# Sums of weight blocks in a seven-product scheme: accumulating transfers in place of VectorE additions

## The chip, the cores and the metric

One NeuronCore of a Trainium2 chip runs the whole kernel. The time is the device time of one execution in microseconds, the median of the runs on the chip. Beside the runs one execution was taken by the hardware profiler; its trace gives the span from the first to the last instruction, and the busy and idle time of each engine: PE (TensorE), PEld (its weight loads), DVE (VectorE), ACT (ScalarE), POOL (GpSimd), and SP, which here only issues transfers.

## The reference

A decoder layer on 528 positions (16 meta tokens and 512 tokens) of width 2048, all in float32:

```python
xn = rmsnorm(h, g_pre)
p = xn @ w_in                       # 2048 x 7184 columns
q, k, v, z_gla, r, hc, gate_b, gate_c, z_conv = jnp.split(p, SPLIT_POINTS, axis=-1)
log_a = jax.nn.log_sigmoid(r @ w_gate_up + b_gate) / GATE_TAU
o = gla_chunked(q * GLA_HEAD_K ** -0.5, k, v, log_a)     # 4 heads, chunks of 64 positions
y_gla = rmsnorm(o, g_gla_out) * silu(z_gla)
y_conv = gate_b * causal_dwconv(gate_c * hc, w_conv) * silu(z_conv)
y = jnp.concatenate([y_gla, y_conv], axis=-1) @ w_out
out = (h + rmsnorm(y, g_post))[N_META:]
```

Most of the arithmetic is in the product with `w_in`, and the next largest part in that with `w_out`.

## The kernel before

**Splitting.** Float32 operands are multiplied in three passes. `split` makes two tiles of a raw block: `whi`, a cast on ACT (L124), and `wlo`, the raw block less `whi`, on DVE (L125). Then TensorE multiplies high by high, high by low and low by high. There are three buffers of `whi` and of `wlo`.

**Pairs.** The columns of `w_in` lie in DRAM as tiles of 128 columns (`w_t`). After some plain products at the start, the rest is done by 25 objects `Pair`: two tiles of 128 columns (such as h4 and c4, whose PSUM tiles are named `h4c4P...`) against all of `xn`, by a scheme of seven block products instead of eight. A pair has four blocks of weights of 128 x 1024 float32, 512 KB each: `"11"` and `"12"`, the halves over the contraction of the first tile, and `"21"` and `"22"`, those of the second. The seven products are made in the order P5, P1, P6, P2, P3, P7, P4, each of 24 matmuls (8 steps of contraction by three passes). Their weight operands are sums of blocks:

- P5: 21 + 22
- P1: 11
- P6: 11 + 21 + 22
- P2: 12
- P3: 11 + 12 + 21 + 22
- P7: 11 + 21
- P4: 22

The sums of `xn` on the other side are made once, ahead of the pairs. The pairs stand in this order: nine for z, k, q and v, then h0c0 and b0s0 (in these eleven the work of the gated attention, the "stages", is interleaved), then fourteen more for the convolution group, h1c1, b1s1 to h7c7, b7s7. Then comes `w_out`: `Whole` and six `Out`, which have their own sums of blocks.

**Slots and loads.** Raw blocks lie in five slots. `load_free` issues the next load of the list on SP's queue whenever a slot is free; `free` gives a slot back once the last instruction that reads it has been written. Four blocks of a pair and the first of the next pair are held when a pair begins.

**Order of the work.** `line` lists all products. The main loop prepares two products ahead (`AHEAD = 2`): `prepare_next` calls `Pair.prepare`, which issues the additions and the split of one product; `multiply` issues its matmuls; `away` takes finished products out of PSUM with copies on ACT and subtractions on DVE. Each engine runs its instructions in the order in which the program, after the framework's scheduling, has written them. In `prepare`, three sums are made by `add` on DVE (L200) and the fourth by a subtraction (L230), all in place in the raw slots:

```python
if name == "P5":   add(raw["21"], raw["22"])
elif name == "P6": add(raw["11"], raw["21"])
elif name == "P3": add(raw["12"], raw["11"])
elif name == "P7": raw["11"] = raw["11"] - raw["22"]     # L230
```

POOL does a few memsets, masks and one small product, and issues no transfers.

Of the kernel before, what the change touches and what calls it, by code (L numbers as in the profile page):

```python
# [13 lines left out]
ALU = mybir.AluOpType  # L14
# [18 lines left out]
NB = 8  # L33
# [12 lines left out]
def hymba_kernel(ctx, tc, xT, x, g_pre, w_r, w_t, w_up, b_gate, g_gla, w_conv, w_o, g_post, out):  # L46
    nc = tc.nc
# [17 lines left out]
    V, A, G = nc.vector, nc.scalar, nc.gpsimd  # L65
# [54 lines left out]
    def split(raw, shape, pool=None):  # L120
        pool = pool or wp
        hi = pool.tile(shape, F32R, tag="whi", name="whi")
        lo = pool.tile(shape, F32R, tag="wlo", name="wlo")
        A.copy(hi, raw)  # L124
        V.tensor_tensor(out=lo, in0=raw, in1=hi.bitcast(F32), op=ALU.subtract)  # L125
        return hi, lo
# [5 lines left out]
    def new_raw(shape=None):  # L132
        tag = slots.pop(0)
        t = wp.tile(shape or [P, NB, P], F32, tag=tag, name="raw", bufs=1)
        held[id(t)] = (t, tag)
        return t

    def free(t):
        slots.append(held.pop(id(t))[1])
# [47 lines left out]
    line = []  # L187
    ready = []
# [10 lines left out]
    def add(a, b):  # L199
        V.tensor_tensor(out=a, in0=a, in1=b, op=ALU.add)  # L200

    class Pair:
# [6 lines left out]
                line.append((self, name, name == ORDER[-1]))  # L209
            loads.extend((self, b) for b in self.blocks)  # L210

        def load(self, b):

            r = self.raw[b] = new_raw()
            g = NB * (b in ("12", "22"))
            i = TILE[self.na if b[0] == "1" else self.nb]
            nc.sync.dma_start(r, w_t[i][:, g:g + NB, :])

        blocks = ("21", "22", "11", "12")

        def prepare(self, name):
            raw = self.raw
            if name == "P5":
                add(raw["21"], raw["22"])
            elif name == "P6":
                add(raw["11"], raw["21"])
            elif name == "P3":
                add(raw["12"], raw["11"])
            elif name == "P7":
                V.tensor_tensor(out=raw["11"], in0=raw["11"], in1=raw["22"], op=ALU.subtract)  # L230
            b = {"P5": "21", "P1": "11", "P6": "11", "P2": "12", "P3": "12", "P7": "11",
                 "P4": "22"}[name]
            two = split(raw[b], [P, NB, P])
            if name in ("P6", "P3", "P7", "P4"):
                free(raw[{"P6": "21", "P3": "12", "P7": "11", "P4": "22"}[name]])
            return two

        def multiply(self, name, two):
# [53 lines left out]
    def load_free():  # L292
        while slots and loads:
            p, b = loads.pop(0)
            p.load(b)

    def prepare_next():
        p, name, last = line[len(ready)]
        load_free()
        ready.append(p.prepare(name))  # L300
        load_free()

# [347 lines left out]
    with tc.tile_pool(name="ini", bufs=1, reuse_waits="tile") as ini:  # L650
# [13 lines left out]
        for n_, (k0, k1) in enumerate(XCUT):  # L664
            ks = slice(k0, k1)
            nc.sync.dma_start(xr[:, ks, :], xT[:, ks, :])
            for kt in range(k0, k1):
                xt, xk = raw_x(kt)
                src = xr[:, kt, :].rearrange("p (s t) -> p s t", t=XHALF)
                A.activation(xt[0][:, :, xk, :], src, AF.Copy, scale=gp[:, kt:kt + 1])  # L670
                V.scalar_tensor_tensor(out=xt[1][:, :, xk, :], in0=src, scalar=gp[:, kt:kt + 1],
                                       in1=xt[0][:, :, xk, :].bitcast(F32),
# [7 lines left out]
            if k0 == 0:  # L680
# [3 lines left out]
                                in1=wr2[:, :, 0:RANK].bitcast(F32), op=ALU.subtract)  # L684
# [28 lines left out]
        for raw in (wk[1][2], wq_[0][2], wq_[1][2]):  # L713
# [5 lines left out]
                        op=ALU.subtract)  # L719
# [35 lines left out]
        def want_plain(n):  # L755
            if n in plain and n not in grans:
# [9 lines left out]
                        op=ALU.subtract)  # L766
# [51 lines left out]
        free(stage[0])  # L818
        all_pairs()
        prepare_next()  # L820
        prepare_next()
        block("P1", xa, 0, b11)
        block("P4", xa, 1, tt)
        multiply(0)
        prepare_next()
        block("P2", xb, 0, b21)
        multiply(1)
# [241 lines left out]
```

## Time and profile before

| | |
|---|---|
| median of 3 runs | 821.43 us (820.8 to 821.86) |
| profiled execution | 823.31 us, span 820.8 us |
| granted TensorE clock, mean | 0.990 |
| busy: PE, DVE, ACT, POOL | 794.0, 688.4, 437.6, 3.8 us |
| moved by DMA | 98.97 MB, mean 121 GB/s |
| 512 KB loads of `w_t` | 108, median 4.1 us from issue to landing |
| stages: start and plain products; 25 pairs; `w_out` | 0 to 99; 99 to 639; 639 to 821 us |

In the rows of groups, the first number after the bar is the busy time of all instructions of the group, then the mean of one in ns; after the second bar stands the idle time of the engine just before them and what ended most of it. In rows of the chain and the timeline the first number is the start in us, the second the length. A row names the line, the engine, the operation, and output and inputs; `x168` is a count.

### The profile page before, as it was taken

The page shows a single profiled execution, that of the slowest core. Times are in us where ns is not written, and L with a number is a line of the kernel's source. Part 1 is how long each engine was busy: PE and PEld are TensorE (multiplying, and loading weights), DVE is VectorE, ACT ScalarE, POOL GpSimd, SP SyncE. Part 2 cuts the span into 40 slices and gives each one's busy share as a digit, 9 for nine tenths or more (in the row PEclk, how much of TensorE's full clock was granted, in tenths as well). Part 3 has the DMA queues.
Part 4 walks back from the last instruction along what each step waited for, and adds up shares of the span by engine and source line. Part 5 has one row for each costly group of instructions (what it writes and reads, how often), then busy time and mean ns, then how long its engine had stood idle before and what let it go on. Part 6 is the DMA issues. An engine that isn't in the chain of part 4 may idle for free.

```text
span 820.8 us, 15178 instructions
## 1 busy us (share of the span) xinstructions
PE 794.0 (97%) x6364; PEld 776.2 (95%) x6364; DVE 688.4 (84%) x820; ACT 437.6 (53%) x638; POOL 3.8 (0%) x15
## 2 busy tenths in 40 slices
PE   9999989999999999999999999999999999999992
PEld 8999989998999999999999999999999889999992
DVE  6999979789697789878887888787879986787887
ACT  7635675685766484644444444444446534444442
POOL 0000000000000000000000000000000000000000
PEclk9999999999999999999999999999999999999996
DMA  9513243234133532253333333333333622333346
GB/s 288 223 52 91 92 129 102 89 119 154 54 103 114 169 99 88 85 193 103 111 105 119 100 116 106 115 102 110 105 115 116 178 77 76 104 101 106 103 161 250
DMA packets 34052, 98.97 MB, mean 121 GB/s; under 512 B 4064, under 2 KB 8800, under 8 KB 33344
## 3 DMA queue, kind: packets, MB, share of 16 engines
q1 hardware_dynamic: 31968, 94.73, 35.7%
q10 hardware_dynamic: 2016, 3.29, 1.2%
q8 instruction: 49, 0.80, 0.4%
q14 instruction: 19, 0.16, 0.1%
HBM read 89.61 MB, written 8.39 MB: 119 GB/s over the span
## 4 chain that ended last, share of the span: by engine, by line
PE 77%; DVE 12%; DMA 4%; ACT 4%; issue 2%; SPq 0%; DVEq 0%; ACTq 0%
PE out L63 5%; PE out3P L63 4%; PE out1P L63 4%; PE out2P L63 3%; PE v L63 3%; PE v2v3P L63 3%; PE h0c0P L63 2%; PE h5c5P L63 2%; PE h2c2P L63 2%; PE h7c7P L63 2%; PE h6c6P L63 2%; PE h4c4P L63 2%; PE h3c3P L63 2%; PE h1c1P L63 2%; PE b0s0P L63 2%; PE b6s6P L63 2%
## 5 line engine op out<-in xcount | busy, mean ns | idle before, releaser
L124 ACT CAST whi<-raw 128x1024 fp32r<-128x1024 f32 x225 | 235.2, 1050 | 256.7 <-DVE raw L200 85.4
L125 DVE TENSOR_TENSOR wlo<-raw,whi 128x1024 fp32r<-128x1024 f32 x225 | 273.7, 1220 | 66.7 <-ACT whi L124 61.5
L200 DVE TENSOR_TENSOR raw<-raw 128x1024 f32<-128x1024 f32 x75 | 90.3, 1219 | 6.6 <-DMA raw<-in_w_t_dram 5.6
L230 DVE TENSOR_TENSOR raw<-raw 128x1024 f32<-128x1024 f32 x25 | 30.5, 1220 | 0.6
L145 ACT CAST whi<-raw 128x1024 fp32r<-128x1024 f32 (+2 forms) x13 | 10.9, 845 | 19.5 <-PE v L63 12.8
L63 PE MATMUL out<-whi,xt 128*128 128x512 f32 x64 | 20.0, 394 | 0.0
L63 PE MATMUL out2P<-whi,xt 128*128 128x256 f32 x96 | 17.2, 282 | 0.4 <-ACT whi L124 0.4
L63 PE MATMUL out3P<-whi,xt 128*128 128x256 f32 x96 | 17.2, 282 | 0.4 <-ACT whi L124 0.4
L63 PE MATMUL out1P<-whi,xt 128*128 128x256 f32 x96 | 17.1, 281 | 0.0
L63 PEld LDWEIGHTS out2P<-whi,xt 128*128 128x128 f32 x96 | 14.7, 188 | 0.6 <-ACT whi L124 0.6
L63 PEld LDWEIGHTS out3P<-whi,xt 128*128 128x128 f32 x96 | 14.7, 188 | 0.6 <-ACT whi L124 0.6
L63 PEld LDWEIGHTS out<-whi,xt 128*128 128x128 f32 x64 | 12.0, 188 | 2.8
L63 PEld LDWEIGHTS out1P<-whi,xt 128*128 128x128 f32 x96 | 14.7, 188 | 0.0
L63 PE MATMUL out2P<-wlo,xt 128*128 128x256 f32 x48 | 13.4, 280 | 0.0
L63 PE MATMUL out3P<-wlo,xt 128*128 128x256 f32 x48 | 13.4, 280 | 0.0
L63 PE MATMUL out1P<-wlo,xt 128*128 128x256 f32 x48 | 13.4, 280 | 0.0
L63 PE MATMUL out<-wlo,xt 128*128 128x512 f32 x32 | 12.6, 394 | 0.0
L146 DVE TENSOR_TENSOR wlo<-raw,whi 128x1024 fp32r<-128x1024 f32 (+2 forms) x13 | 12.5, 965 | 0.0
L605 DVE SCALAR_TENSOR_TENSOR y<-hh,wc,y 128x512 f32<-128x512 f32 x16 | 12.0, 748 | 0.2
L363 ACT ACTIVATE junk<-y 128x256 f32<-128x256 f32 x18 | 7.5, 418 | 8.7 <-DVE y L474 8.4
L63 PE MATMUL out3P<-whi,xb 128*128 128x256 f32 x64 | 11.7, 282 | 0.0
L63 PE MATMUL out2P<-whi,xb 128*128 128x256 f32 x64 | 11.6, 282 | 0.0
(749 smaller groups left out, 2701.3 us busy)
## 6 DMA issues: line engine op xcount, KB each, us to landing
raw<-in_w_t_dram SPq DMA_DIRECT2D x108, 512.0 KB, 4.1
raw<-in_w_o_dram SPq DMA_DIRECT2D x24, 512.0 KB, 4.0
raw<-in_w_o_dram SPq DMA_DIRECT2D x16, 256.0 KB, 3.5
xres<-in_x_dram SPq DMA_DIRECT2D x4, 1024.0 KB, 8.0
xr<-in_xT_dram SPq DMA_DIRECT2D x7, 528.0 KB, 6.9
z<-zd SPq DMA_DIRECT2D x8, 256.0 KB, 3.9
yd<-z SPq DMA_DIRECT2D x8, 256.0 KB, 2.0
yg<-yd SPq DMA_DIRECT2D x1, 2048.0 KB, 10.2
```

Of the source, the lines that this page charges most:

```text
L63: nc.tensor.matmul(out_, lhsT, rhs, start=start, stop=stop, **kw)
L124: A.copy(hi, raw)
L125: V.tensor_tensor(out=lo, in0=raw, in1=hi.bitcast(F32), op=ALU.subtract)
L145: A.copy(hi[:, k, :], raw[:, k, :])
L146: V.tensor_tensor(out=lo[:, k, :], in0=raw[:, k, :], in1=hi[:, k, :].bitcast(F32), op=ALU.subtract)
L200: V.tensor_tensor(out=a, in0=a, in1=b, op=ALU.add)
L230: V.tensor_tensor(out=raw["11"], in0=raw["11"], in1=raw["22"], op=ALU.subtract)
L363: A.activation(junk, oy["src"], AF.Square, accum_out=fin["ssq"][:, t, n:n + 1])
L605: V.scalar_tensor_tensor(out=y, in0=hh[:, i:i + S], scalar=wc[:, j, i:i + 1], in1=y, op0=ALU.mult, op1=ALU.add)
```

## The change

In the pairs the four sums are no longer made by DVE. In their place POOL issues transfers from DRAM that add the block they bring to what lies in a slot (`accum_op`), so the block is read from DRAM a second time. With names for the four transfers of a pair:

- F (`first_sum`): 22 is added to slot 21, which gives P5's operand. It is issued two products after the load of block 21 was issued, which is in the pair before, or at P5 at the latest.
- A1: after P5's split, 11 is added to slot 21, which gives P6's operand.
- A2: after P1's split, 21 is added to slot 11, which gives P7's operand (in place of the subtraction).
- A3: after P6's split, 12 is added to slot 21, which gives P3's operand.

The loads of a pair come in the order 21, 11, 12, 22 instead of 21, 22, 11, 12, and the slots are given back at P2, P3, P7 and P4 instead of P6, P3, P7 and P4.

```diff
-        blocks = ("21", "22", "11", "12")
+        def load(self, b):
+            r = self.raw[b] = new_raw()
+            nc.sync.dma_start(r, self.src(b))
+            if b == "21":
+                self.sum_due = len(ready) + 2
+
+        def add_block(self, o, b):
+
+            G.dma_start(self.raw[o], self.src(b), accum_op=ALU.add)
+
+        def first_sum(self):
+            if self.sum_due is not None:
+                self.sum_due = None
+                self.add_block("21", "22")
+
+        blocks = ("21", "11", "12", "22")
+        sum_due = None
 
         def prepare(self, name):
             raw = self.raw
             if name == "P5":
-                add(raw["21"], raw["22"])
-            elif name == "P6":
-                add(raw["11"], raw["21"])
-            elif name == "P3":
-                add(raw["12"], raw["11"])
-            elif name == "P7":
-                V.tensor_tensor(out=raw["11"], in0=raw["11"], in1=raw["22"], op=ALU.subtract)
-            b = {"P5": "21", "P1": "11", "P6": "11", "P2": "12", "P3": "12", "P7": "11",
+                self.first_sum()
+            b = {"P5": "21", "P1": "11", "P6": "21", "P2": "12", "P3": "21", "P7": "11",
                  "P4": "22"}[name]
             two = split(raw[b], [P, NB, P])
-            if name in ("P6", "P3", "P7", "P4"):
-                free(raw[{"P6": "21", "P3": "12", "P7": "11", "P4": "22"}[name]])
+            if name == "P5":
+                self.add_block("21", "11")
+            elif name == "P1":
+                self.add_block("11", "21")
+            elif name == "P6":
+                self.add_block("21", "12")
+            else:
+                free(raw[b])
             return two
...
     def prepare_next():
         p, name, last = line[len(ready)]
         load_free()
+        for q in dict.fromkeys(e[0] for e in line):
+            if getattr(q, "sum_due", None) == len(ready):
+                q.first_sum()
         ready.append(p.prepare(name))
```

Three pieces of the engines' order show what moved. First VectorE in the conv pairs, before, from the split of P1 of pair h4c4 to the split of its P3. `raw_5292`, `raw_5457`, `raw_5491` and `raw_5392` are its blocks 21, 11, 12 and 22, `raw_5524` and `raw_5622` are 21 and 22 of the next pair, b4s4:

```order
L125 TENSOR_TENSOR wlo_5585<-raw_5457,whi_5584 128x1024 [waits DMAHW0_49,Activation_49]
L200 TENSOR_TENSOR raw_5457<-raw_5457,raw_5292 128x1024 [waits DVE_49]
L261 TENSOR_TENSOR sg_5518<-v_5581,b3s3P4_5588 128x256 [waits PE_49]
L125 TENSOR_TENSOR wlo_5619<-raw_5457,whi_5618 128x1024 [waits Activation_49]
L625 TENSOR_TENSOR yc_4226<-y_5383,sg_5518 128x512 [waits Activation_49]
L125 TENSOR_TENSOR wlo_5652<-raw_5491,whi_5651 128x1024 [waits DMAHW1_49,PE_49,Activation_49]
L200 TENSOR_TENSOR raw_5524<-raw_5524,raw_5622 128x1024 [waits DMAHW3_49,DMAHW2_49]
L200 TENSOR_TENSOR raw_5491<-raw_5491,raw_5457 128x1024 [waits DVE_49]
L230 TENSOR_TENSOR raw_5457<-raw_5457,raw_5392 128x1024 [waits DVE_49]
L125 TENSOR_TENSOR wlo_5684<-raw_5491,whi_5683 128x1024 [waits PE_49,Activation_49]
```

The four additions of a pair stand between the splits, that of the next pair's P5 among them. The same place on VectorE in the changed kernel, where `raw_5293`, `raw_5426` and `raw_5459` are blocks 21, 11 and 12 of h4c4:

```order
L125 TENSOR_TENSOR wlo_5586<-raw_5426,whi_5585 128x1024 [waits DMAHW7_49,Activation_49]
L276 TENSOR_TENSOR sg_5519<-v_5582,b3s3P4_5590 128x256 [waits PE_49]
L125 TENSOR_TENSOR wlo_5621<-raw_5293,whi_5620 128x1024 [waits DMASW5_49,Activation_49]
L643 TENSOR_TENSOR yc_4228<-y_5385,sg_5519 128x512 [waits Activation_49]
L125 TENSOR_TENSOR wlo_5653<-raw_5459,whi_5652 128x1024 [waits DMAHW0_49,PE_49,Activation_49]
L125 TENSOR_TENSOR wlo_5686<-raw_5293,whi_5685 128x1024 [waits DMASW0_49,PE_49,Activation_49]
```

The additions are gone, and the splits of P6 and P3 wait for `DMASW...`, the semaphores of POOL's transfers. POOL's own queue around the same pair, with `raw_5525` for block 21 of b4s4 and `raw_5755` for that of h5c5:

```order
L226 DMA raw_5293<-in_w_t_dram 128x1024 [waits DMASW2_49,DVE_49]
L226 DMA raw_5525<-in_w_t_dram 128x1024 [waits DMAHW5_49,DMAHW2_49,DMASW7_49]
L226 DMA raw_5426<-in_w_t_dram 128x1024 [waits DMAHW4_49,DMAHW7_49,DMASW0_49,DVE_49]
L226 DMA raw_5293<-in_w_t_dram 128x1024 [waits DMASW5_49,DVE_49]
L226 DMA raw_5525<-in_w_t_dram 128x1024 [waits DMASW6_49,DVE_49]
L226 DMA raw_5755<-in_w_t_dram 128x1024 [waits DMAHW6_49,DMAHW1_49,DMASW3_49]
```

These rows are A1 of h4c4, F of b4s4, A2 and A3 of h4c4, A1 of b4s4 and F of h5c5: each waits on its own engine's queue for the transfer that filled the slot and, but for F, for the VectorE half of a split that reads it.

More of the change, by code (lines that the diff above doesn't have):

```diff
@@ L210, in __init__, with src @@
             loads.extend((self, b) for b in self.blocks)
+        def src(self, b):
+            g = NB * (b in ("12", "22"))
+            i = TILE[self.na if b[0] == "1" else self.nb]
+            return w_t[i][:, g:g + NB, :]
         def load(self, b):
             r = self.raw[b] = new_raw()
-            g = NB * (b in ("12", "22"))
-            i = TILE[self.na if b[0] == "1" else self.nb]
-            nc.sync.dma_start(r, w_t[i][:, g:g + NB, :])
-        blocks = ("21", "22", "11", "12")
+            nc.sync.dma_start(r, self.src(b))
[9 more added lines that the diff above has]
+        sum_due = None
         def prepare(self, name):
```

## The prediction

> **What bounds the kernel now.** I read the page's first lines, then the chain that ended last, then the windows by stage.
>
> ```profile
> span 820.8 us, 15178 instructions
> PE 794.0 (97%) x6364; PEld 776.2 (95%) x6364; DVE 688.4 (84%) x820; ACT 437.6 (53%) x638; POOL 3.8 (0%) x15
> ...
> 438.79 20.20 PE h3c3P L63 x168
> 458.99 19.90 PE b3s3P L63 x168
> ```
>
> TensorE is busy 97% of the span. From 358.58 to 639.28 us the chain holds nothing but TensorE: one pair after another, 168 products back to back, 20.20 and 19.90 us in turn (mean 20.05, or 2.86 per product of the seven and 0.12 per matmul). Fourteen pairs lie there. VectorE is at 84%, but what its work is worth has to be read by stage:
>
> ```profile
> 97.00:122.00 25.00, 21.99 (x181) 21.56 (x179) 20.06 (x22) 18.16 (x25) 0.00 (x0) 1.00 0.39 127
> 122.00:210.00 88.00, 86.97 (x698) 84.85 (x699) 73.93 (x106) 56.30 (x97) 0.00 (x0) 0.98 0.35 109
> 210.00:300.00 90.00, 87.12 (x710) 84.80 (x710) 73.59 (x95) 62.21 (x96) 0.00 (x0) 1.00 0.32 106
> 300.00:345.00 45.00, 43.98 (x364) 42.85 (x363) 41.69 (x57) 27.15 (x48) 0.00 (x0) 1.00 0.31 94
> 358.58:639.28 280.70, 280.70 (x2354) 280.70 (x2353) 235.61 (x262) 131.25 (x162) 0.00 (x0) 1.00 0.35 111
> ```
>
> Columns: stretch, its length, then busy time of PE, PEld, DVE, ACT, POOL, the granted clock, the share of the DMA engines, GB/s. In the last row TensorE is busy for the whole stretch at clock 1.00: nothing taken from VectorE can shorten it. In the four rows before, TensorE lacks 3.01, 1.03, 2.88 and 1.02 us: 7.9 us is all that a relieved VectorE could win among the pairs.
>
> **What is removed.** Four VectorE additions in each of 25 pairs (L200 three times, L230 once):
>
> ```profile
> L124 ACT CAST whi<-raw 128x1024 fp32r<-128x1024 f32 x225 | 235.2, 1050 | 256.7 <-DVE raw L200 85.4
> L125 DVE TENSOR_TENSOR wlo<-raw,whi 128x1024 fp32r<-128x1024 f32 x225 | 273.7, 1220 | 66.7 <-ACT whi L124 61.5
> L200 DVE TENSOR_TENSOR raw<-raw 128x1024 f32<-128x1024 f32 x75 | 90.3, 1219 | 6.6 <-DMA raw<-in_w_t_dram 5.6
> L230 DVE TENSOR_TENSOR raw<-raw 128x1024 f32<-128x1024 f32 x25 | 30.5, 1220 | 0.6
> ```
>
> That is 120.8 us of VectorE, 4.9 per pair, hidden behind TensorE except for a part of the 7.9 us. The split of a block (cast L124, then subtraction L125) stays: 1.05 and 1.22, some 2.3 with the hand-over.
>
> **What is added.** 100 accumulating transfers of 512 KB issued from POOL, four a pair. I call them F (block 22 onto slot 21, before P5), A1 (block 11 onto slot 21, after P5's split), A2 (21 onto slot 11, after P1's split) and A3 (12 onto slot 21, after P6's split). POOL's order in the conv pairs is A1, then the next pair's F, A2, A3. F and A2 have several products of time. A1 and A3 do not: slot 21 serves P5, P6 and P3, which stand two products apart. So there is a new chain in each pair: split of P5, A1, split of P6, A3, split of P3. How much time it has, the rows of one pair tell (two engines; start, duration):
>
> ```profile
> 450.28 1.05 ACT L124 CAST whi<-raw 128x1024 fp32r<-128x1024 f32 x1 [1.66 <-PE h3c3P L63]
> 453.13 1.05 ACT L124 CAST whi<-raw 128x1024 fp32r<-128x1024 f32 x1 [1.52 <-PE h3c3P L63]
> 454.22 1.23 DVE L125 TENSOR_TENSOR wlo<-raw,whi 128x1024 fp32r<-128x1024 f32 x1 [0.54 <-ACT whi L124]
> 456.01 1.05 ACT L124 CAST whi<-raw 128x1024 fp32r<-128x1024 f32 x1 [1.83 <-PE h3c3P L63]
> 458.36 1.22 DVE L200 TENSOR_TENSOR raw<-raw 128x1024 f32<-128x1024 f32 x1
> 459.69 1.05 ACT L124 CAST whi<-raw 128x1024 fp32r<-128x1024 f32 x1 [2.63 <-DVE raw L200]
> ```
>
> The casts at 450.28, 453.13 and 456.01 are those of P4 and of the next pair's P5 and P1. Each ends a wait for TensorE: there are three buffers, so the cast of a product starts when TensorE has finished the product three before. P5's split ends at 455.45. P3 of that pair starts on TensorE at 458.99 + 4 x 2.84 = 470.35 (19.90 / 7 a product), and its cast must start 2.06 earlier (2.3 less the two matmuls of 0.12 that need no low half), at 468.3. In between lie A1, one split and A3, so **A1 + A3 <= 468.3 - 455.45 - 2.3 = 10.55 us** costs nothing. Above that the loop closes on itself: from P3's cast the split and 22 more matmuls (2.3 + 2.6 = 4.9) end the product whose buffer the next P5 needs, so a pair takes 4.9 + 2.3 + A1 + 2.3 + A3 = 9.5 + A1 + A3.
>
> **What one such transfer takes.** The kernel before has none, and none from POOL. The nearest rows are the plain loads of the same block in conv pairs (400 to 600 us: packets, MB, share; then issue to landing) and the longest transfer:
>
> ```profile
> q1 hardware_dynamic: 5760, 20.97, 32.4%
> ...
> raw<-in_w_t_dram SPq DMA_DIRECT2D x40, 512.0 KB, 4.1
> ...
> DMA to landing us min/median/max: 3.5/4.1/5.3
> ...
> yg<-yd SPq DMA_DIRECT2D x1, 2048.0 KB, 10.2
> ```
>
> 40 loads hold 16 engines for 32.4% of 200 us: 64.8 us, 1.62 each; the other 2.5 of the 4.1 is fixed. (The 2 MB row agrees: 6.1 us for 1.5 MB more, 2.0 per block.) An accumulating transfer reads the source and also the slot, then writes the slot. Lower bound: the slot's read hides, 4.1 landing and 1.62 of engines. Upper: the three movements follow each other, 4.1 + 3.24 = 7.3 and 4.86. I take one extra pass, being nearest to what the operation needs over a load (one more operand): **5.7 to land, 3.24 of engines**. POOL's own share of an issue has no row; I take it as what SP's load has within its 4.1, and keep 1 us more for the range.
>
> [...]
>
> The engines are shared. With A1 issued at 0 it lands at 5.7; F and A2, queued behind it, at 8.9 and 12.2. P6's split ends at 5.7 + 2.3 = 8.0, where A3 is issued; alone it would land at 13.7, behind A2 at 15.4. So A3 is 7.4. The SP load into the slot that P2 frees falls on it too (1.62 of engines): up to 9.0, and I take 8.2. Pair: 9.5 + 5.7 + 8.2 = 23.4 us.
>
> **The sum.** Conv pairs: 14 x (23.4 - 20.05) = +47. The eleven pairs before, with the group work among them, run from 99.33 to 358.58:
>
> ```profile
> 95.45 1.21 DVE raw L200
> ...
> 99.33 2.89 PE z2z3P L63 x22
> ```
>
> 23.6 us a pair. TensorE is busy 21.99 + 86.97 + 87.12 + 43.98 there up to 345 us and the 13.6 to 358.58, in all 253.7; less 11 x 20.05 that leaves 33 us of group work, 3 a pair; half of it in the new chain gives 24.9, +1.3 each, +14. First pair: the addition at 95.45 lies on the chain right ahead of a product, and A3 of 5.7 stands in place of 1.2: +4. VectorE's relief counts 0 here, since casts wait for transfers. Queues: SP loses nothing (blocks are loaded in another order, into slots freed up to two products later, each still a pair ahead); POOL held nothing in the pairs that anyone waits for. w_o's stages are unchanged. Total +65. The profiled execution took 823.31 us (span 820.8 and 2.5 around it), 0.2% above the median of 821.43; on that median **886 us**, on the profiled one 888.
>
> **Rivals.**
> *Hidden transfers (the other side).* If the slot's read overlaps the source's, a transfer lands in 4.1, engines take 1.62 and A3 meets no queue: A1 + A3 = 8.2 < 10.55. TensorE stays the bound in the conv pairs; elsewhere relief wins up to the 7.9 us, I say 4: 817, or 821 if the chain's remaining waits eat it. It decides at 5.3 us per transfer, not far from 4.1. For it: the loads' engine share of 0.35 leaves room. Against: 5.3 is also the slowest plain load, and four more transfers at 1.62 would bring the engines to 65%.
> *Half hidden.* 4.9 landing, 2.4 of engines: A3 lands at 12.2 after issue at 7.2, 5.0, with the load 5.8; the pair takes 20.2: +2, first pair +3: 826.
> *The engines as bound.* Three movements: A1 7.3, F 12.2, A2 17.1, A3 21.9 after issue at 9.6: 12.3, with the load 13.1; pair 29.9: 14 x 9.85 + 11 x 7.8 + 8 = +232: 1053. For it: two passes already hold the engines 4 x (1.62 + 3.24) = 19.4 of 20.05 us.
>
> **How the numbers follow.** One extra pass 0.50, its own range 857 (A3 7.4, no group work in the chain: 14 x 2.55) to 955 (each issue 1 us dearer and all group work in the chain: 14 x 5.35 + 11 x 4.8 + 6). Half hidden 0.15 (822 to 857). Engines as bound 0.17. Hidden 0.18, half of it with a gain. A measurement of this kernel tells about 0.2% from no change. Slower 0.82, same 0.09, faster 0.09. The range leaves out the gain and the upper part of the dearest case: 820 to 1000.
>
> **What would show it.** VectorE's busy time near 568 us and no L200 or L230 of this shape among pairs; casts of P6 and P3 that wait for a DMA into raw by some us each, that of P3 longer; conv pairs of 23.4 us on the chain with TensorE idle inside each; DMA share about 0.8 there; SP's loads landing later than 4.1. Wrong would be conv pairs still of 20.05 (landing under 5.3), pairs of 28 or more (engines full), or POOL taking over 1 us per issue before the engines start.

## The result, and the profile after

The changed kernel takes **938.37 us** (median of 4 runs, 933.66 to 943.4) against 821.12 for the kernel before on the same chip: ratio 1.1417 [1.1388, 1.1446]. The profiled execution took 933.66 us, its span is 931.7.

The page's first lines and the shares of the chain that ended last:

```profile
span 931.7 us, 15386 instructions
PE 834.4 (90%) x6364; PEld 806.4 (87%) x6364; DVE 574.6 (62%) x720; ACT 429.5 (46%) x638; POOL 90.9 (10%) x115
...
DMA 37%; PE 29%; DVE 12%; issue 11%; ACT 10%; POOL 1%; SPq 0%; DVEq 0%; ACTq 0%; POOLq 0%
```

VectorE lost 113.8 us of work and the span became 110.9 us longer. The chain is led by transfers, where before the conv pairs were TensorE alone. A second thing to see: TensorE makes the same 6364 matmuls and is busy 40.4 us more.

Groups of instructions:

```profile
L125 DVE TENSOR_TENSOR wlo<-raw,whi 128x1024 fp32r<-128x1024 f32 x225 | 273.4, 1222 | 257.4 <-ACT whi L124 253.4
L124 ACT CAST whi<-raw 128x1024 fp32r<-128x1024 f32 x225 | 231.6, 1046 | 401.3 <-DMA raw<-in_w_t_dram 231.6
L226 POOL DMA_DIRECT2D raw<-in_w_t_dram x100 | 87.6, 900 | 624.5 <-DVE wlo L125 330.6
```

Before, VectorE's additions ended the largest part of the casts' waits (85.4 of 256.7 us, in the row that the prediction shows); now transfers into the slots do (231.6 of 401.3 us). POOL, idle before, spends 0.9 us on each issue.

Where the time went, by the first matmul of a tile (from the rows by tile; "early" are the ten pairs from k1q1 to h1c1, "conv" the fourteen from h1c1 to `w_out`):

| | before | after |
|---|---|---|
| k1q1 starts | 107.7 | 107.8 |
| h1c1 starts (ten early pairs) | 358.4 (25.1 a pair) | 411.9 (30.4 a pair) |
| `w_out` starts (fourteen conv pairs) | 639.1 (20.05 a pair) | 750.0 (24.15 a pair) |
| end of the span | 820.8 | 931.7 |

So +53.4 us lie in the early pairs, +57.4 in the conv pairs, and nothing ahead of or behind them. The first of the 25 pairs, z2z3, is not among the ten. In the kernel before it starts at 86.4 us, so the pairs begin there and not at 99 (rows of its tile and of the second pair's: first and last start of these matmuls):

```profile
L63 PE MATMUL z2z3P<-xt,whi x48: 278/280/387, 86.4 to 104.7; 128*128 128x256 f32 x48
```
```profile
L63 PE MATMUL k1q1P<-xt,whi x48: 278/283/290, 107.7 to 129.1; 128*128 128x264 f32 x48
```

Stretches of one early and of the conv stage in the changed kernel (columns as in the prediction):

```profile
200.00:300.00 100.00, 84.95 (x649) 81.27 (x648) 53.25 (x79) 53.80 (x95) 11.38 (x13) 0.95 0.68 160
...
448.00:750.00 302.00, 275.05 (x2143) 268.64 (x2142) 159.38 (x192) 113.64 (x147) 41.95 (x48) 0.95 0.77 178
```

In the second row TensorE, which was never idle there before, is idle for 27 us, runs at a granted clock of 0.95, and the DMA engines are at 0.77. One conv pair on the chain (start, length, what; P6's split, A3, P3's split, P3's product, the next P5's split, A1):

```profile
564.45 1.06 ACT whi L124
565.53 1.24 DVE wlo L125
566.77 0.40 issue
567.16 5.72 DMA raw<-in_w_t_dram
572.92 0.04 issue
572.96 1.05 ACT whi L124
574.03 1.24 DVE wlo L125
575.27 0.04 issue
575.32 4.21 PE h4c4P L63 x21
579.55 1.06 ACT whi L124
580.63 1.24 DVE wlo L125
581.87 0.39 issue
582.27 5.62 DMA raw<-in_w_t_dram
```

This is the loop that the prediction drew: split, transfer, split, transfer, split, and one product that closes it. The `x21` piece is too long: 21 matmuls at 0.12 are 2.5 us, not 4.2. TensorE's own rows there (start, length, matmuls of P3; two of `whi` in a row):

```profile
574.06 0.51 PE L63 MATMUL h4c4P<-xb,whi 128*128 128x258 f32 x2 [0.78 <-ACT whi L124]
575.32 0.39 PE L63 MATMUL h4c4P<-xb,wlo 128*128 128x258 f32 x1 [0.76 <-DVE wlo L125]
575.54 0.40 PE L63 MATMUL h4c4P<-xb,whi 128*128 128x258 f32 x2
...
576.30 0.63 PE L63 MATMUL h4c4P<-xb,whi 128*128 128x258 f32 x2
...
579.94 0.40 PE L63 MATMUL h4c4P<-xt,whi 128*128 128x258 f32 x2
```

After two pauses of 0.78 and 0.76 us, while P3 waited for its split, the matmuls follow at 0.12, then from 576.2 to 579.5 at 0.215, then at 0.12 again. The granted clock over 572 to 580 us is 0.79.

Transfers between 500 and 700 us (packets, MB, share of 16 engines; then the median from issue to landing):

```profile
q0 software_dynamic: 4680, 17.01, 48.2%
q1 hardware_dynamic: 5116, 18.66, 28.5%
...
raw<-in_w_t_dram SPq DMA_DIRECT2D x35, 512.0 KB, 5.3
raw<-in_w_t_dram POOLq DMA_DIRECT2D x33, 512.0 KB, 6.4
```

A transfer of POOL's is 144 packets (14400 in the whole run, by 100); 4680 are 32.5 of them in 96.4 us of 16 engines, 2.97 each.

### The profile page after: what moved, and what is told of

Read it like the earlier page. It is cut to its first block, busy times and chain, and to the rows that moved or that the text cites. A ratio compares the mean times of both kernels' runs of the same rounds, so it can differ in the third digit from the quotient of the medians.

```text
span 931.7 us, 15386 instructions
## 1 busy us (share of the span) xinstructions
PE 834.4 (90%) x6364; PEld 806.4 (87%) x6364; DVE 574.6 (62%) x720; ACT 429.5 (46%) x638; POOL 90.9 (10%) x115
## 3 DMA queue, kind: packets, MB, share of 16 engines
q0 software_dynamic: 14400, 52.44, 32.2%
## 4 chain that ended last, share of the span: by engine, by line
DMA 37%; PE 29%; DVE 12%; issue 11%; ACT 10%; POOL 1%; SPq 0%; DVEq 0%; ACTq 0%; POOLq 0%
DMA raw<-in_w_t_dram 37%; DVE wlo L125 7%; ACT whi L124 6%; PE out L63 5%; PE out3P L63 3%; PE out1P L63 3%; PE out2P L63 3%; PE v L63 3%; PE z L63 2%; PE b7s7P L63 1%; PE b4s4P L63 1%; PE z2z3P L63 1%; DVE y L586 1%; PE b0s0P L63 1%; ACT junk L381 1%
## 5 line engine op out<-in xcount | busy, mean ns | idle before, releaser
L124 ACT CAST whi<-raw 128x1024 fp32r<-128x1024 f32 x225 | 231.6, 1046 | 401.3 <-DMA raw<-in_w_t_dram 231.6
L226 POOL DMA_DIRECT2D raw<-in_w_t_dram x100 | 87.6, 900 | 624.5 <-DVE wlo L125 330.6
L63 PE MATMUL o<-st,ed 128*128 128x256 f32 x48 | 10.2, 312 | 7.6 <-ACT st L867 7.6
L63 PEld LDWEIGHTS o<-st,ed 128*128 128x128 f32 x48 | 8.0, 211 | 8.2 <-ACT st L867 8.2
L63 PE MATMUL k3q3P<-xb,whi 128*128 128x264 f32 x32 | 8.0, 349 | 6.4 <-ACT q L286 6.4
L63 PE MATMUL k2q2P<-xt,whi 128*128 128x264 f32 x48 | 11.0, 327 | 2.7 <-ACT whi L124 2.7
L63 PE MATMUL k1q1P<-xt,whi 128*128 128x264 f32 x48 | 10.6, 318 | 2.1 <-ACT whi L124 2.1
```

The lines of the kernel that those rows point to most:

```text
L63: nc.tensor.matmul(out_, lhsT, rhs, start=start, stop=stop, **kw)
L226: G.dma_start(self.raw[o], self.src(b), accum_op=ALU.add)
```

## The experiments

All are timed in rounds against the kernel before on the same chip. Early and conv pairs are read as above.

| kernel | median us | ratio to before | early pair | conv pair |
|---|---|---|---|---|
| before | 821.12 | 1 | 25.1 | 20.05 |
| changed | 938.37 | 1.1417 [1.1388, 1.1446] | 30.4 | 24.15 |
| e1_filler | 1002.74 | 1.2195 [1.2152, 1.2238] | 31.3 | 28.2 |
| e2_copy | 842.02 | 1.0212 [1.0165, 1.0258] | 26.7 | 20.6 |
| e3_far | 823.68 | 1.0013 [1.0002, 1.0024] | 25.1 | 20.05 |
| e4_near | 924.02 | 1.1241 [1.12, 1.1282] | 28.6 | 24.3 |
| e5_pinned | 921.06 | 1.1189 [1.1133, 1.1245] | 28.6 | 23.9 |
| e6_pinned_fill | 930.45 | 1.1327 [1.1283, 1.1371] | 30.4 | 23.4 |
| e7_spread | 910.84 | 1.1079 [1.1045, 1.1113] | 28.3 | 23.7 |
| e8_before_spread | 823.0 | 0.9998 [0.9983, 1.0013] | 24.9 | 20.1 |
| e9_three_steps | 866.85 | 1.053 [1.0501, 1.056] | 26.7 | 21.7 |
| e10_fill_last | 870.27 | 1.0573 [1.0555, 1.059] | 26.1 | 22.6 |
| e11_three_transfers | 833.42 | 1.013 [1.0113, 1.0147] | 25.5 | 20.3 |

### Is it the chain, and is the addition its price?

Three edits of the changed kernel, each leaving a part of it: plain copies in place of adding transfers (the sums are left out, so what it computes is not the layer); only F and A2 as transfers; only A1 and A3.

**e2_copy**

```diff
-            G.dma_start(self.raw[o], self.src(b), accum_op=ALU.add)
+            G.dma_start(self.raw[o], self.src(b))
```

> The 100 transfers from POOL are plain copies onto the same slots (no sum is made), with the same waits. Theory 1 with the second pass as the price: 16 engines held 1.6 us instead of 3.0 by each, landing 6.4 -> 5.0, conv pairs 24.15 -> 20.5 to 21.3, the kernel 850 to 875 us. Rival (the fixed part and POOL's issue are the price, not the addition): landing stays over 6.0 and the kernel over 915 us.

Measured: 842.02 us, a little under the range. The page's rows:

```profile
q0 software_dynamic: 14400, 52.44, 19.3%
...
L226 POOL DMA_DIRECT2D raw<-in_w_t_dram x100 | 53.1, 531 | 572.6 <-DVE wlo L125 342.6
...
raw<-in_w_t_dram POOLq DMA_DIRECT2D x100, 512.0 KB, 4.9
```

The same bytes without the addition hold 16 engines for 1.63 us a transfer (19.3% of 844.6 us, by 100); with it 3.00 (32.2% of 931.7), 1.84 times as long. They land in 4.9 instead of 6.7 us, and POOL issues one in 0.53 instead of 0.90. Waits, queues and slots are the same, so the addition is worth 96 of the 117 us.

**e3_far**: F and A2 stay transfers, the sums of P6 and P3 are VectorE's again (A1 and A3 are the lines taken out; A2 is issued behind the sum of P6, which reads block 11 as it was loaded).

```diff
             if name == "P5":
                 self.first_sum()
+            elif name == "P6":
+                add(raw["21"], raw["11"])
+                self.add_block("11", "21")
+            elif name == "P3":
+                add(raw["21"], raw["12"])
+                free(raw["12"])
...
-                self.add_block("21", "11")
...
-                self.add_block("21", "12")
```

> F and A2 (the two with several products of time) stay transfers; the sums of P6 and P3 (A1, A3) go back to VectorE. Theory 1 (the chain of A1 and A3 is the whole cost): conv pairs 20.05, the kernel 814 to 822 us, VectorE some 60 us less busy than before. Rival (accumulating traffic as such, by full engines or POOL's waits, delays the loads): DMA share near 0.6 in the conv pairs, loads over 5 us late enough to stall TensorE, 830 us or more.

**e4_near**: A1 and A3 stay transfers, P5's sum and P7's operand are VectorE's again (blocks loaded in the old order; A2 is the line taken out).

```diff
             if name == "P5":
-                self.first_sum()
+                add(raw["21"], raw["22"])
+            elif name == "P6":
+                V.tensor_tensor(out=raw["11"], in0=raw["21"], in1=raw["22"], op=ALU.subtract)
...
-                self.add_block("11", "21")
```

> A1 and A3 stay transfers; F and A2 go back to VectorE (P7's operand as P6's less block 22). Theory 1: the chain stays, A1 and A3 land in 5.4 to 5.8 as they already do in conv pairs, conv pairs 23.5 to 24.2; only the eleven pairs before gain, where A1 is queued behind F: the kernel 905 to 930 us. Rival (shared engines and queue are the cost): with half the accumulating traffic conv pairs fall under 21.5 and the kernel under 880 us.

Measured: 823.68 us, 1.7 above the range of theory 1 and clear of the rival's, and 924.02 us, in theory 1's range. Half of the transfers cost nothing that matters (0.1%), and the other half nearly everything. Of e3_far the page's busy line and issues:

```profile
PE 794.5 (97%) x6364; PEld 777.6 (95%) x6364; DVE 631.8 (77%) x770; ACT 435.5 (53%) x638; POOL 47.2 (6%) x65
...
raw<-in_w_t_dram POOLq DMA_DIRECT2D x50, 512.0 KB, 5.8
```

Fifty transfers of 5.8 us are hidden when nobody needs them soon, and 56.6 us less of VectorE bring nothing. In e4_near half the adding traffic gives the conv pair of the full change (24.3 against 24.15), so there it is the chain through slot 21 and not the load of the engines.

### Is the clock part of it, and POOL's order?

**e1_filler**: 18 throwaway matmuls ahead of P3, into the bank that P7 will overwrite, to keep TensorE busy through the pause.

```diff
+            if name == "P3":
+                sp = self.sb["P7"] = bank(f"{self.na}{self.nb}P7")[:, 0:w]
+                for i in range(18):
+                    mm(sp, xh[:, s, 0, 0:P], xl[:, s, i % NB, c0:], True, True)
```

> 18 matmuls of 0.12 us (2.2 us), whose results are thrown away, stand on TensorE right ahead of P3's, where it waits for the transfer A3. Theory 1 (chain of A1 and A3, and TensorE runs P3's matmuls at half rate after the gap of some 2.3 us, 4.2 us instead of 2.6): no slow stretch, conv pairs 24.15 -> 22.6 us, the kernel 900 to 918 us. Rival (the slow matmuls are not set by the gap, or the cast of the next P5 waits for something else): conv pairs stay at 24.1 or longer, 935 to 950 us.

Measured: 1002.74 us, a miss for both. The edit moved more than it should: the scheduler put F ahead of A1 on POOL in twelve conv pairs too. Its rows (two engines; x3 are F, A1 and A2, then P6's cast):

```profile
592.00 2.66 POOL L226 DMA_DIRECT2D raw<-in_w_t_dram  x3 [16.66 <-DVE wlo L125]
...
600.52 1.04 ACT L124 CAST whi<-raw 128x1024 fp32r<-128x1024 f32 x1 [10.07 <-DMA raw<-in_w_t_dram]
```

A1 behind F, and A2 right behind both, make P6's cast wait 10.07 us where 4.6 stood in the changed kernel: in these pairs A1 is issued 1.8 to 4.8 us after the end of P5's split, where 0.4 is usual, because F, ahead of it, is issued only 0.7 us after the load of its block has landed. The pair is 4 us longer; how much of it is the filler itself this run can't tell, nor does it say anything on the clock. But it pointed to the early pairs, where the changed kernel has the same order in six of the ten (so POOL's rows and the landings show; the expectation of e5 below takes it for all). One of the six (the end of P5's split on VectorE; then the chain of the changed kernel):

```profile
226.36 1.22 DVE L125 TENSOR_TENSOR wlo<-raw,whi 128x1024 fp32r<-128x1024 f32 x1
```
```profile
222.57 3.56 DMA raw<-in_w_t_dram
...
226.80 0.86 POOL raw L226
...
227.99 7.73 DMA raw<-in_w_t_dram
235.75 0.04 issue
235.79 1.06 ACT whi L124
```

A load lands at 226.1, then F is issued, then A1 at 227.99: 0.4 us after the end of P5's split (227.58), so here F did not hold its issue. But A1 lands only after 7.73 us, with F's transfer right ahead of it. Over the six pairs with F ahead A1 takes 7.0 to 9.9 us to land and its issue is held by up to 1.0; in the four others it takes 5.5 to 6.7.

**e5_pinned**: POOL's issues kept in written order, F one product later, so A1, A2, A3, F (and 7 PSUM banks, as e6 needs them).

```diff
-                self.sum_due = len(ready) + 2
+                self.sum_due = len(ready) + 3
...
-            G.dma_start(self.raw[o], self.src(b), accum_op=ALU.add)
+            tc.keep_in_program_order(
+                G.dma_start(self.raw[o], self.src(b), accum_op=ALU.add))
```

> POOL's queue is held in the order A1, A2, A3, then the next pair's F, in all pairs (in the changed kernel F stands ahead of A1 in the eleven pairs before the convolution group); one PSUM bank less is used. Theory 1b (A1 behind F costs some 2 us a pair in the early pairs; nothing in the conv pairs): conv pairs stay at 24 us, early pairs fall from 28.4 to about 26.5, the kernel 910 to 925 us. Rival (POOL's order is of no account; the early pairs lose to their group work): 933 to 945 us.

**e6_pinned_fill**: e5 with 18 throwaway matmuls into the eighth bank ahead of P3.

```diff
+            if name == "P3":
+                for i in range(18):
+                    mm(fillb[:, 0:w], xh[:, s, 0, 0:P], xl[:, s, i % NB, c0:], True, True)
```

> As e5_pinned, with 18 matmuls of 0.12 us into the spare bank right ahead of P3's in every pair, so that TensorE doesn't idle there. Theory 1 (after the gap TensorE runs P3 at half rate, 4.2 us instead of 2.6): conv pairs 1.3 to 1.6 us shorter than in e5_pinned, the kernel 15 to 30 us faster than e5_pinned, at a higher granted clock. Rival (the slow matmuls are no part of the chain): same as e5_pinned or up to 20 us slower.

e5 met its range: 921.06 us, and h1c1 starts at 395.9 instead of 411.9. So F ahead of A1 was worth 1.8 us an early pair; A1's landing, in the mean of the ten 7.3 us in the changed kernel and 5.9 in e5, is most of it, and e4, which has no F on POOL, comes to the same 28.6. The rest of the early cost, 3.5 us a pair, stays, and one pair of e5 shows what the group work does there (three engines; P5's cast, the end of its split, A1's issue):

```profile
247.68 1.03 ACT L124 CAST whi<-raw 128x1024 fp32r<-128x1024 f32 x1
...
250.47 1.22 DVE L125 TENSOR_TENSOR wlo<-raw,whi 128x1024 fp32r<-128x1024 f32 x1
...
252.09 0.86 POOL L227 DMA_DIRECT2D raw<-in_w_t_dram  x1 [18.85 <-DVE v L301]
```

The split takes 4.0 us, not 2.3: between cast and subtraction VectorE runs the attention's rows, which stand ahead in its order. Group work is in the chain there.

e6 came out 9 us slower than e5, not faster: the rival's range. The filler did its work on the clock; the conv stage of e5 (first) and e6:

```profile
395.90:731.80 335.90, 306.49 (x2361) 299.39 (x2360) 175.88 (x211) 127.37 (x163) 47.28 (x54) 0.94 0.80 180
```
```profile
417.10:747.30 330.20, 319.00 (x2612) 314.22 (x2611) 175.62 (x210) 126.38 (x163) 47.25 (x54) 0.99 0.81 181
```

The clock goes from 0.94 to 0.99, and the interval from P3's cast to the next P5's is 5.2 to 5.7 us in twelve pairs one after another, 5.3 in the mean; in the same twelve pairs of e5 the mean is 6.1, and in the changed kernel, where it is 6.1 too, seven of the twelve take 6.5 to 7.3 (the casts from 437.30 to 720.94 us) and the other five 5.2. The pair shrinks by 0.45 us only, since the two intervals that hold the transfers grow by 0.3 together. In the early pairs the filler is bare work. So the slow clock is a small part of the conv pairs' cost, 0.45 us a pair by this run and at most the 0.9 that the interval lost, and not its cause.

### Can another order hide the transfers?

**e7_spread**: POOL pinned, F two products later, and another order of products. **e8_before_spread**: the kernel before in that order, its additions moved to fit. In both, the first pair adds P2 onto P1's bank before P1 is copied out.

```diff
-ORDER = ("P5", "P1", "P6", "P2", "P3", "P7", "P4")
+ORDER = ("P1", "P5", "P2", "P6", "P7", "P4", "P3")
```

> The changed kernel with the products in the order P1, P5, P2, P6, P7, P4, P3 and POOL's queue in program order: P5 and P6 are still two products apart, P6 and P3 three. The time for A1 + A3 grows from 10.55 by one product to 13.4 us, where they take 11.4 to 12.2. Theory 1 (the chain): conv pairs back at 20.05 to 20.6, the kernel 818 to 840 us. Rival (engines full): the 16 engines need 18.4 us of each pair, so at 20.05 they are 92% busy, transfers queue and land later, conv pairs 21 to 23, the kernel 850 to 890 us.

> Control: the kernel before (sums on VectorE) with the same order of products P1, P5, P2, P6, P7, P4, P3. Either theory: TensorE stays the bound, 817 to 828 us; if it is over 830, the order itself costs something that has to be taken off the reading of e7_spread.

Measured: 910.84 us, a miss for both theories; e8 823.0, so the order as such costs nothing. The reason in e7 is on ACT:

```profile
569.74 1.04 ACT L124 CAST whi<-raw 128x1024 fp32r<-128x1024 f32 x1 [3.34 <-DMA raw<-in_w_t_dram]
570.69 0.37 ACT L287 COPY q<-b4s4P 128x256 f32<-128x256 f32 x1
```

P2's product adds onto P1's bank and so waits for the copy `q`; `q` stands on ACT behind P6's cast, and that waits for A1. The transfer holds two products at once. That is how the chain runs in ten of the fourteen conv pairs; in the other four the next P5's cast waits for F, which is issued right behind A3 and lands 9.6 to 11.5 us later.

**e9_three_steps**: POOL pinned, three products' time on either side of P6, and two products between P1 and P2 (P4's result is taken away with P7's).

```diff
-ORDER = ("P5", "P1", "P6", "P2", "P3", "P7", "P4")
+ORDER = ("P5", "P1", "P4", "P6", "P2", "P7", "P3")
...
-                self.sum_due = len(ready) + 2
+                self.sum_due = len(ready) + 3
```

> All 100 accumulating transfers stay; the products go P5, P1, P4, P6, P2, P7, P3, so that three products' time (3 x 2.86 = 8.6 us) lies from P5's cast to P6's and from P6's to P3's, and the copy of P1 out of its bank has two products' time before P2 adds to it. GpSimd issues A1, A2, F, A3 in this order. If the chain through slot 21 alone set the time (split 2.3 + transfer about 6.2 = 8.5 us, as it was in the changed kernel), it now just fits: conv pairs of 20.1 to 20.8 us, 820 to 845 us in all. Rival, the transfer engines: a pair needs 4 x 3.0 + 4 x 1.6 = 18.4 us of all 16 of them in 20.05, landings grow as the gaps close, conv pairs of 21.5 us or more and 850 to 890 us, with the casts of P6 and P3 still waiting for transfers.

Measured: 866.85 us and 21.7 a conv pair, in the rival's range. All 100 transfers are still there, so 71 of the 117 us went with the order of the products and of POOL's queue (17 of them with the queue's alone, by e5). What is left, one pair in stretches (A1 is issued at 529.8, A3 at 539.3 and lands at 548.4):

```profile
530.00:536.60 6.60, 6.60 (x58) 6.60 (x58) 5.20 (x8) 1.78 (x2) 2.40 (x3) 1.00 0.96 179
536.60:540.00 3.40, 3.40 (x31) 3.40 (x30) 2.31 (x2) 2.58 (x5) 0.68 (x1) 1.00 0.98 199
540.00:548.50 8.50, 8.23 (x70) 8.03 (x68) 1.79 (x3) 1.01 (x1) 0.20 (x1) 1.00 0.90 259
548.50:552.40 3.90, 2.01 (x14) 1.81 (x15) 2.75 (x4) 3.21 (x4) 0.02 (x1) 1.00 0.11 33
```

The engines are full (0.96, 0.98, 0.90) from A1's issue to A3's landing, then idle (0.11) until the next P5's split releases the next burst, although over the stage they are at 0.82.

**e10_fill_last**: e9 with `len(ready) + 4`, so F behind A3. **e11_three_transfers**: e9 with F as a VectorE addition again.

```diff
             if name == "P5":
-                self.first_sum()
+                add(raw["21"], raw["22"])
```

> The kernel of three steps with one change: GpSimd issues A1, A2, A3, F, so that F stands behind A3 and not ahead of it. In the three-step kernel 16 engines were 0.96 to 0.98 busy from A1's issue on, and A3 (issued 539.32) landed 9 us later, behind A2, F and the loads. If that queue, and not a chain of bare landings, holds P3's cast, A3 now lands 2 to 3 us sooner, a conv pair takes 19.9 to 20.8 us instead of 21.67 and the whole 830 to 852 us. Rival: the pair's traffic as a whole is the limit (18.4 us of engines, and bursts); then F only takes the wait over at P5's cast, and it stays at 860 to 875 us.

> The three-step order again, with A1, A2 and A3 as transfers and F back on VectorE (one addition of 128x1024 ahead of P5's split): the chain through slot 21 is the same, the pair's transfers need 3 x 3.0 + 4 x 1.6 = 15.4 us of the 16 engines and not 18.4. If the engines' share sets the three-step kernel's 21.67 us a conv pair, it now falls to 20.1 to 20.6 us and the whole to 822 to 840 us, with A3's landing back at 5 to 6.5 us. Rival: the chain with its late issues (A1 2.9 us behind P5's cast, A3 2.7 us behind P6's) sets it, and it stays at 855 to 870 us.

e10 took 870.27 us, as its rival said: A3 now lands 6.2 us after its issue instead of 8.2 (medians of twelve conv pairs), and P5's cast waits for F instead. On its chain F, issued right behind A3, takes

```profile
515.83 11.24 DMA raw<-in_w_t_dram
```

e11 took 833.42 us, as expected for the engines: by the sum in its expectation the pair's transfers hold them 15.4 us instead of 18.4, and in most of its conv pairs the chain is TensorE's again.

```profile
508.50 20.00 PE b4s4P L63 x168
528.50 20.22 PE h5c5P L63 x168
```

A3's landing came back to 5.8 us (median of the same twelve pairs), as expected; A1's is 7.2, and in most pairs neither is on the chain. The run takes F's landing away together with its engine time, so it doesn't part the two. No version here beats the kernel before: the best are e3_far and e11, the one 0.1% slower and the other 1.3%.

## Why the prediction was right, and where not

The sign and the mechanism were right: 886 us predicted, 938.37 measured, inside the range (820 to 1000, which is wide) and 52 us above the value. The cost was 117 us where 65 was said. By its steps:

- **VectorE's relief counts nothing.** Right: 574.6 us busy where 568 was said, and e3_far shows 56.6 us of relief that bring nothing.
- **One extra pass: 5.7 us to land, 3.24 of engines.** Right in kind and near in size: 5.62 and 5.72 on the chain, 3.00 of engines against 1.63 for a copy. That the operation moves one more operand, and how the movements follow each other inside a transfer, was my estimate; the runs show only what a whole transfer takes. "Hidden" fell on both terms. "Half hidden" had 4.9 and 2.4, "engines as bound" 7.3 and 4.86; the load of the engines set the time only in e9 and e10, by late landings, once the chain had been given room.
- **The conv pair as 9.5 + A1 + A3 = 23.4.** 23.6 between the casts at 437.30 and 720.94 us (twelve pairs), 24.15 with the pairs at both ends. The sum hides three errors. From P5's cast to P6's the mean is 8.8 where 2.3 + 5.7 = 8.0 was said; 0.4 of that is the step from VectorE to POOL ahead of each transfer (the `issue` rows of 0.40 and 0.39), which the sum lacks. From P6's to P3's it is 8.75 where 2.3 + 8.2 = 10.5 was said: A3 is issued 8.4 us after A1 (582.27 and 590.70), when the queue of F and A2 is nearly through, and it lands in 6.0 us in the mean of the twelve where 8.2 was said. From P3's cast to the next P5's it is 6.1 where 4.9 was said: the clock, which I left out, is at most 0.9 of it. The first conv pair took 31.0 (406.31 to 437.30): its A1 took 9.9 us to land, beside the 2 MB transfer `yg<-yd`, which was under way from 404.4 to 416.7, and its A3 8.8, right behind F, which had waited for a late load until 421.16. In all +57 instead of +47.
- **The early pairs, +14, and the first pair, +4.** This is the step that failed: +53. Three things in it were wrong. First the reading of before: 99.33 us, where the sum lets eleven pairs begin, lies in the middle of the first, z2z3 (86.4 to 107.7). So ten pairs run from 107.7 to 358.4, 25.1 us each and not 23.6, with 5.0 us of group work each and not 3. Then the choice "half of the group work in the new chain": in e5, without F ahead of A1, an early pair takes 28.6, which is its conv pair of 23.9 and 4.7 of group work on top. So nearly all of the group work adds to the chain and gives the transfers next to no cover, and an early pair loses 3.5 us, about what a conv pair loses (3.9 in e5). (With the prediction's own 23.4 and all 5.0 on top it would have been +3.3 a pair, +33. Its upper bound of 4.8 a pair is 2.8 with all of its 3 us of group work, and 2 for dearer issues.) Last the order of POOL's queue, which adds another 1.8 in the changed kernel and which no bound held; I read the order of the conv pairs (A1 first) and took it for all. The first pair cost nothing: k1q1 starts at 107.8 as before.
- **POOL's share of an issue.** Taken as part of the landing; it takes 0.9 us of POOL, and the landings of 5.6 to 5.7 count from its start. Right to leave it out of the sum.
- **Signs.** DMA share 0.77 where 0.8 was said, casts waiting for transfers, TensorE idle in each conv pair, SP's loads at 5.1 instead of 4.1: all there. "That of P3 longer" is so by half a microsecond only: over the twelve conv pairs P3's cast waits 5.35 us in the mean and P6's 4.86, where the sum made A3 2.5 us longer than A1.

Left open: which engine's group work (TensorE's, VectorE's or ACT's) keeps an early pair from hiding the transfers. That nearly all of it adds to the chain is arithmetic on the pairs' times, and no run took any of it away. e5 also issues F one product later and has one PSUM bank less; these were not tried one by one.

## What to carry to other kernels

In this kernel an adding transfer in place of a VectorE addition traded 1.2 us of VectorE for some 6 us of latency (5.6 to 5.7 on the chain of the conv pair shown, 6.7 in the median of all 100) and 3 us of all DMA engines. It was free where its result was wanted several products later and the engines had room (e3_far, ratio 1.0013; q0 and q1 hold them for 18.3% and 35.2% of its span), and it lost time where each result feeds the next one (e4_near, ratio 1.1241), although the relieved engine was 84% busy. First look whether the engine relieved ends any wait in the stage, then count the transfers in series, then the engine time of all transfers in one period; and read the order on the issuing queue in every stage, not in one.

## What the runs showed of the hardware

- Adding to what lies in the slot (the changed kernel) cost 1.84 times the engine time of a copy (e2_copy): 3.00 against 1.63 us for 512 KB. It took 0.90 against 0.53 us of POOL per issue, and 6.7 against 4.9 us to land (median of 100).
- In the changed kernel TensorE went from 0.12 to 0.215 us a matmul for 3.3 us (576.2 to 579.5, granted clock 0.50 over 576.3 to 579.5), after two pauses of 0.78 and 0.76 us; seven of twelve pairs show the same longer interval (6.5 to 7.3 us from P3's cast to the next P5's, 5.2 in the others). The next two pairs have pauses of 0.64 and 0.76 us (b4s4, 597 to 599) and of 1.96 and 0.76 us (h5c5, 620 to 622) at the same place, and the granted clock is 1.00 there (595 to 602 and 618 to 625). So the length of these pauses does not tell whether the slow stretch comes; what starts and ends it was not shown. With matmuls in the pause the granted clock of the conv stage was 0.99 (e6_pinned_fill) instead of 0.94 (e5_pinned).
- The mean share of the DMA engines did not tell whether they set the time: at 0.82 in the conv stage of e9 a pair took 21.7 us, at 0.79 in e11 20.3, nearly TensorE's pace. In the pair of e9 shown, the chain releases the transfers at nearly one time (shares of 0.90 to 0.98 while they stand) and leaves the engines idle in between (0.11).
